# Moving the release of an expert's weight splits to GpSimd, and a second buffer for the rows of every other expert

## The chip, the cores and the metric

The kernel runs on one core of a Trainium2 chip. The metric is the device time of that core in microseconds (us), from launch to end. The profile is one execution of the same program, taken by the hardware profiler. Engines: TensorE (PE, with its weight loads as PEld), VectorE (DVE), ScalarE (ACT), GpSimd (POOL) and SyncE (SP, which issues the direct DMAs).

## The reference, cut to what matters

Two transformer layers over 512 tokens of width 1024 (with 256 context tokens). The second one ends in a mixture of eight experts, two for each token. All of the change lies in this last part:

```
def swiglu(x, w1, w3, w2):
    return (jax.nn.silu(x @ w1) * (x @ w3)) @ w2

def moe_swiglu(x, router, w1, w3, w2):
    ...
    logits = (xt @ router).astype(jnp.float32)
    top_v, top_i = lax.top_k(logits, TOP_K)
    top_w = jax.nn.softmax(top_v, axis=-1)
    gates = jnp.sum(jax.nn.one_hot(top_i, N_EXPERTS, dtype=jnp.float32) * top_w[..., None], axis=1)
    ...
    out = gates[:, 0:1] * swiglu(xt, w1[0], w3[0], w2[0])
    for e in range(1, N_EXPERTS):
        out = out + gates[:, e:e + 1] * swiglu(xt, w1[e], w3[e], w2[e])
```

w1, w3 are 1024x1408 and w2 is 1408x1024 for each expert. The result of the layer is the residual plus the gated output.

## The kernel before

**Weights.** Every matrix product is made of three float16 products: a float32 weight is scaled by 1024 and split into a high part (ACT, L283) and a low part (DVE, L288). A block of weights is a 128x2048 tile of w1 and w3 (11 of them for an expert, written j0 to j10 here) or a 128x1408 tile of w2 (8 of them, d0 to d7), so 19 blocks for an expert. `Stream` moves the blocks through two sets of buffers. A staging slot holds the float32 block as SP's DMA brings it (L260); it comes free when DVE has made the low part, and SP, which issues in order, then loads the next block into it. Before the change there are eight staging slots in this part: h (3), Kd (2), wst (2), Qc (1), named after the tensors whose space they use. A split slot holds the two float16 parts: whi/wlo (4), whix/wlox (1), aT (3). Splits run five blocks ahead of the block that TensorE multiplies (`LS1`). The first blocks of the first expert are split in four quarters of 512 columns.

**Experts.** They are taken in eight fixed places e0 to e7 with room for 176, 192, 96, 176, 112, 152, 136 and 128 tokens (e0 is expert 0, the others are ranked by load). `route` computes the top two, a position for every token, the one-hot matrices (ohs, L1707), from them by TensorE the token numbers (idxps, L1715), and as integers idx. `gather(e)` has GpSimd fetch an expert's tokens by indirect DMA into xg (one DMA for each group of up to 128 tokens, two for most experts). `prep` transposes xg on TensorE (xtp, L1858) and makes the float16 parts xT; for e0 it selects by one-hot matmuls instead (L1854), so that e0 needs no gather. `expert` runs the 11 blocks of w1 and w3 (L356), then the 8 of w2; the result comes back through ACT (my), a transpose (ytp) and DVE, which multiplies by the gate into the row buffers yr (L1927). `add_rows` has GpSimd add the finished rows into the output in DRAM by an indirect DMA (L2085). These DMAs follow each other: each waits until the one before it has landed. The tiles yr exist once (one for each group of tokens), so an expert's first rows wait until the DMAs of the expert before have read them.

**Order.** The order of instructions on each engine is decided at build time by the framework's scheduler, from data dependences and the order in which the code emits them; on the chip each engine then runs its list in that order and waits at the head of it. One dependence is put in by hand: for the first splits that `expert` asks for in e0 (j3 to j5 come under it), ACT's scale is not the constant 1024 but a tile `sw` that holds 1024, so that they can't be scheduled before `sw` is written:

```
        self.S.scale = self.ms.tile([128, 1], F32, name="sw")
        V.tensor_scalar(self.S.scale, pm[:, 0, 0:1], 0.0, SW, op0=OP.mult, op1=OP.add)
```

pm (L1691) holds the tokens' positions, which are known early in `route`. The blocks j0 to j2 and j7 are split before `route`.

Of the kernel before, what the change touches and what calls it, by code (L numbers as in the profile page):

```python
# [11 lines left out]
F32 = mybir.dt.float32  # L12
F16 = mybir.dt.float16
# [3 lines left out]
OP = mybir.AluOpType  # L17
# [4 lines left out]
D = 1024  # L22
# [12 lines left out]
CM = max(CAPS)  # L35
# [24 lines left out]
SW = 1024.0  # L60
# [146 lines left out]
def fixed_slot(kind, name, z):  # L207

    return kind, name, [z.bitcast(F32)] if kind == 'st' else [z[:, 0:2 * D], z[:, 2 * D:4 * D]]
# [110 lines left out]
class K:  # L320
# [1309 lines left out]
    def route(self, rp, pp, hook):  # L1630
        nc = self.nc
        V = nc.vector
# [19 lines left out]
        def t3(nm, dt=F32):  # L1652
            return rp.tile(b3, dt, name=nm)
# [36 lines left out]
        pm = t3("pm")  # L1690
# [26 lines left out]
        first = slots(0, lambda t: pm[:, t, 0:1])  # L1717

        self.S.scale = self.ms.tile([128, 1], F32, name="sw")
        V.tensor_scalar(self.S.scale, pm[:, 0, 0:1], 0.0, SW, op0=OP.mult, op1=OP.add)  # L1720
        hook([z[:, 0:CAPS[0]] for z in first])

        b77 = [128, 7, 7]
# [53 lines left out]
        for i, (s0, sn) in enumerate(self.slots[1]):  # L1777
            V.tensor_copy(self.idx[0:sn, 1, i:i + 1], ip[0:sn, 1, i, 0:1])
        self.gather(1)

        def rest(j):

# [83 lines left out]
                nc.vector.tensor_tensor(out=xT[:, 1, q, :], in0=af[:, q, :], in1=xT[:, 0, q, :], op=OP.subtract)  # L1866
        return xT

    def expert(self, C, slots, w13, w2, xT, mp, pp, done, wt=None, mid=None, nb=2, cm=CM, midj=6, beside=None):


        nc = self.nc
        CB = 256 if C <= 256 else 512
        gate = self.gate[3]
        gT = self.cut(mp.tile([128, 22 * cm], F16, name="mgT", tag="mgT", bufs=1), 22, C)
        gT = gT.rearrange("p (z k) c -> p z k c", z=2)
        prev, gf = [], [None]

        def evac():
            j, ps = prev.pop(0)  # L1880
            if j % 4 == 0:
                gf[0] = self.cut(mp.tile([128, 4 * cm], F32, name="mgf", tag="mgf", bufs=nb), 4, C)
            s = mp.tile([128, cm], F32, name="ms", tag="ms", bufs=2)[:, 0:C]
            nc.scalar.activation(s, ps[:, 0, 0:C], AF.Silu, scale=DESC)
            nc.vector.scalar_tensor_tensor(out=gf[0][:, j % 4, :], in0=ps[:, 1, 0:C], scalar=DESC * SA, in1=s, op0=OP.mult,  # L1885
                                           op1=OP.mult)
            if j in (3, 7, 10):
                q = slice(j // 4 * 4, j + 1)
                g = gf[0][:, 0:j % 4 + 1, :]
                nc.scalar.activation(gT[:, 0, q, :], g, AF.Copy)  # L1890
                nc.vector.tensor_tensor(out=gT[:, 1, q, :], in0=g, in1=gT[:, 0, q, :], op=OP.subtract)

        seg = [(0, C)]
        for j in range(11):
            wh, wl = (z.rearrange("p (j k c) -> p j k c", j=2, k=8) for z in w13(j))
            self.S.scale = SW
            ps = pp.tile([128, 2, CB], F32, name="mps", tag="m", bufs=3)
            for i in range(2):
                for k in range(KD):
                    self.mm1(ps[:, i], wh[:, i], wl[:, i], k, xT[:, 0], xT[:, 1], seg, k == 0, k == 7)  # L1900
            if prev:
                evac()
            prev.append((j, ps))
            if beside is not None:
                beside(j)
            if j == midj and mid is not None:
                mid()
        evac()
        yr = [mp.tile([128, D], F32, name="yr", tag=f"yr{s}", bufs=1) for s in range(len(slots))]
        py = []  # L1910

        def evac2():
            d, ps = py.pop(0)
            y = mp.tile([128, cm], F32, name="my", tag="my", bufs=nb)[:, 0:C]
            nc.scalar.activation(y, ps[:, 0, 0:C], AF.Copy, scale=gate[:, d, 0:1])  # L1915
            ys.append((d, y))

        def rows():
            d, y = ys.pop(0)
            tp = pp.tile([128, max(2, len(slots)), 128], F32, name="ytp", tag="t", bufs=2)  # L1920
            dd = slice(d * 128, (d + 1) * 128)
            for s, (s0, sn) in enumerate(slots):
                nc.tensor.transpose(tp[0:sn, s, :], y[:, s0:s0 + sn], self.ident)  # L1923
                if wt is None:
                    nc.vector.tensor_copy(yr[s][0:sn, dd], tp[0:sn, s, :])
                else:
                    nc.vector.tensor_scalar(yr[s][0:sn, dd], tp[0:sn, s, :], wt[0:sn, s:s + 1], None, op0=OP.mult)  # L1927
            done(d, yr)

        def part(w, ps, ks):  # L1930
            for k in ks:
                self.mm1(ps[:, 0], *w, k, gT[:, 0], gT[:, 1], seg, k == 0, k == 10)

        ys = []
        w0 = []
        for d in range(8):
            if d > 1 and len(ys) > nb - 1:
                rows()
            w = [z.rearrange("p (k c) -> p k c", k=11) for z in w2(d)]
            ps = pp.tile([128, 2, CB], F32, name="mps2", tag="m", bufs=3)  # L1940
            if d < 2 and nb > 1:

                part(w, ps, range(8))
                w0.append((w, ps))
                if d == 0:
                    continue
                for i in range(2):
                    part(*w0[i], range(8, 11))
                    py.append((i, w0[i][1]))
                evac2()  # L1950
                continue
            part(w, ps, range(11))
            if py:
                evac2()
            py.append((d, ps))
        evac2()
        while ys:
            rows()

    def overflow(self):  # L1960

# [71 lines left out]
    def moe(self, ctx):  # L2033
        nc, tc = self.nc, self.tc

        self.slots = [[(0, C // 2), (C // 2, C // 2)] if C > 128 else [(0, C)] for C in CAPS]
        self.eid = {}
        res = self.A['out'][0:NL].rearrange("(t p) c -> t p c", p=128)
        for t in range(4):
            nc.sync.dma_start(out=res[t], in_=self.h[:, t, :])  # L2040
        self.xg = {}
        with ExitStack() as c0:
            wx = c0.enter_context(tc.tile_pool(name="wx", bufs=1))
            self.S.extend(wx, 0, 1, fixed=self.wfix)
            self.S.ls = 4
            self.xgp = c0.enter_context(tc.tile_pool(name="xgp", bufs=1))
            rp = c0.enter_context(tc.tile_pool(name="rt", bufs=1))
            pp = c0.enter_context(tc.tile_pool(name="pm", bufs=1, space=PSUM))
            with ExitStack() as c:
                mp = c.enter_context(tc.tile_pool(name="mp", bufs=1))  # L2050
                first = []
                rest = self.route(rp, pp, lambda ohs: first.append(self.prep(CAPS[0], self.slots[0], None, mp, pp, ohs=ohs)))
                xT = first[0]

                B = [self.at3[:, 4 * D * z:4 * D * z + 4 * D] for z in range(3)]
                H = [self.ht[:, 2 * D * z:2 * D * z + 2 * D].bitcast(F16) for z in range(3)]
                self.S.extend(wx, 0, 1, fixed=self.wfix + [fixed_slot('hl', f"a{i}", z) for i, z in enumerate(B)]
                              + [fixed_slot('st', f"h{i}", z) for i, z in enumerate(H)])
                self.S.ls = LS1
                for e in range(NE):  # L2060
                    nxt = []

                    def mid():
                        if e + 2 < NE:
                            self.gather(e + 2)
                        if e + 1 < NE:
                            nxt.append(self.prep(CAPS[e + 1], self.slots[e + 1], self.xg.pop(e + 1), mp, pp))

                    self.expert(CAPS[e], self.slots[e], lambda j: self.S.get(('m13', e, j)), lambda j: self.S.get(('m2', e, j)),
                                xT, mp, pp, lambda d, yr: self.add_rows(e, d, yr), self.ws[:, e, :], mid, beside=None if e else rest)  # L2070
                    xT = nxt[0] if nxt else None
        self.kctx.close()
        self.overflow()
# [64 lines left out]
```

## Time and profile before

| | us |
|---|---|
| median of 3 runs | 1798.25 (1798.06 to 1801.5) |
| the profiled execution: its time | 1797.55 |
| its span, first to last instruction | 1795.8 |
| PE busy | 1654.4 (92%) |
| DVE busy | 1244.4 (69%) |
| ACT busy | 882.2 (49%) |
| mean granted TensorE clock | 0.975 |

The profiled execution takes 1.75 us more than its span, for what lies before the first and after the last instruction. The expert part lies between about 1288 us and the end. [...]

### The profile page before, as it was taken

The page shows a single profiled execution, that of the slowest core. Times are in us where ns is not written, and L with a number is a line of the kernel's source. Part 1 is how long each engine was busy: PE and PEld are TensorE (multiplying, and loading weights), DVE is VectorE, ACT ScalarE, POOL GpSimd, SP SyncE. Part 2 cuts the span into 40 slices and gives each one's busy share as a digit, 9 for nine tenths or more (in the row PEclk, how much of TensorE's full clock was granted, in tenths as well). Part 3 has the DMA queues.
Part 4 walks back from the last instruction along what each step waited for, and adds up shares of the span by engine and source line. Part 5 has one row for each costly group of instructions (what it writes and reads, how often), then busy time and mean ns, then how long its engine had stood idle before and what let it go on. Part 6 is the DMA issues. An engine that isn't in the chain of part 4 may idle for free. (4 is left out here: it accounts for less than half of the span.)

```text
span 1795.8 us, 36123 instructions
## 1 busy us (share of the span) xinstructions
PE 1654.4 (92%) x15124; PEld 1164.0 (65%) x15124; DVE 1244.4 (69%) x2397; ACT 882.2 (49%) x1420; POOL 155.0 (9%) x103
## 2 busy tenths in 40 slices
PE   3999999999999999999998999989669999999976
PEld 1444666555556666555555466457569988999976
DVE  6784899777664554233158999696867598787963
ACT  6564555253222222111255677565646587686762
POOL 1100000000000000000001000461130010010211
PEclk8999999999999999999999999999789999999988
DMA  8413242533443332233321202112468889999972
GB/s 324 156 51 108 98 162 95 213 116 141 141 141 139 124 137 96 72 112 112 115 92 60 83 1 72 71 48 90 168 208 306 267 287 359 324 363 326 314 251 48
DMA packets 53736, 286.83 MB, mean 160 GB/s; under 512 B 7760, under 2 KB 12880, under 8 KB 29504
## 3 DMA queue, kind: packets, MB, share of 16 engines
q1 hardware_dynamic: 47328, 271.74, 42.1%
q0 software_dynamic: 5232, 10.96, 2.9%
q8 instruction: 120, 1.97, 0.4%
q10 hardware_dynamic: 1008, 1.77, 0.3%
q14 instruction: 48, 0.39, 0.1%
HBM read 272.57 MB, written 11.08 MB: 158 GB/s over the span
## 5 line engine op out<-in xcount | busy, mean ns | idle before, releaser
L356 PEld LDWEIGHTS <-whi 128*128 128x128 f16 x5120 | 465.0, 98 | 184.5 <-issue 10.4
L356 PE MATMUL f<-yT,whi 128*128 128x512 f16 (+1 forms) x1408 | 325.5, 326 | 1.5 <-ACT af L452 1.5
L356 PEld LDWEIGHTS <-wlo 128*128 128x128 f16 x2560 | 251.7, 98 | 88.1 <-issue 0.4
L356 PE MATMUL f<-yT,wlo 128*128 128x512 f16 (+1 forms) x704 | 229.1, 326 | 0.0
L288 DVE SCALAR_TENSOR_TENSOR wlo<-wst,whi 128x2048 f16<-128x2048 f32 (+2 forms) x113 | 172.3, 1534 | 53.9 <-ACT whi L283 53.7
L283 ACT ACTIVATE whi<-wst 128x2048 f16<-128x2048 f32 (+2 forms) x115 | 147.0, 1299 | 89.0 <-PE f L356 71.9
L389 DVE SCALAR_TENSOR_TENSOR adjk<-wst,srow 128x1024 bf16<-128x1024 f32 x96 | 117.2, 1221 | 99.9 <-DMA wst<-in_w_adr_dram 98.8
L356 PE MATMUL f<-gT,whi 128*128 128x512 f16 (+1 forms) x704 | 164.4, 326 | 0.0
L356 PEld LDWEIGHTS <-aT 128*128 128x128 f16 x2376 | 153.6, 98 | 2.7 <-issue 2.2
L356 PE MATMUL mps<-xT,whi 128*128 128x176 f16 (+6 forms) x1408 | 142.3, 228 | 1.6 <-ACT xT L1865 1.3
L356 PE MATMUL mps<-xT,wlo 128*128 128x176 f16 (+6 forms) x704 | 136.6, 228 | 0.0
L288 DVE SCALAR_TENSOR_TENSOR wlo<-h,whi 128x2048 f16<-128x2048 f32 (+1 forms) x54 | 107.2, 1987 | 21.2 <-ACT whi L283 18.4
L356 PE MATMUL f<-gT,wlo 128*128 128x512 f16 (+1 forms) x352 | 114.7, 326 | 0.0
L283 ACT ACTIVATE whi<-h 128x2048 f16<-128x2048 f32 (+1 forms) x54 | 90.2, 1672 | 48.4 <-PE mps L356 46.6
L356 PE MATMUL mps<-xT,aT 128*128 128x112 f16 (+6 forms) x1584 | 105.5, 225 | 0.0
L481 DVE TENSOR_TENSOR h<-h,ytp 128x256 f32<-128x256 f32 (+1 forms) x48 | 24.3, 506 | 109.6 <-PE ytp L479 109.5
L356 PE MATMUL cvps<-aT,whi 128*128 128x512 f16 (+1 forms) x384 | 82.6, 328 | 2.8 <-ACT Kl L646 2.3
L288 DVE SCALAR_TENSOR_TENSOR aT<-wst,aT 128x2048 f16<-128x2048 f32 (+2 forms) x44 | 76.2, 1749 | 12.5 <-ACT aT L283 12.4
L1096 ACT CAST gT<-g 128x512 f16<-128x512 f32 (+1 forms) x23 | 14.0, 608 | 131.2 <-DVE g L1093 131.2
L356 PE MATMUL mps<-mgT,whi 128*128 128x176 f16 (+6 forms) x704 | 73.2, 229 | 1.4 <-DVE mgf L1885 0.9
L283 ACT ACTIVATE aT<-wst 128x2048 f16<-128x2048 f32 (+2 forms) x40 | 62.3, 1569 | 23.2 <-PE mps L356 22.0
L2085 POOL DMA_INDIRECT out_dram<-yr,sidx x14 | 41.9, 2989 | 336.6 <-DVE yr L1927 184.9
(405 smaller groups left out, 3404.7 us busy)
## 6 DMA issues: line engine op xcount, KB each, us to landing
wst<-in_w_adr_dram SPq DMA_DIRECT2D x32, 1024.0 KB, 4.9
h<-in_w_m_dram SPq DMA_DIRECT2D x30, 1024.0 KB, 9.4
wst<-in_w_m_dram SPq DMA_DIRECT2D x24, 1024.0 KB, 7.1
wst<-in_w_f_dram SPq DMA_DIRECT2D x22, 1024.0 KB, 4.9
Kd<-in_w_m_dram SPq DMA_DIRECT2D x22, 1024.0 KB, 7.2
h<-in_w_m_dram SPq DMA_DIRECT2D x24, 704.0 KB, 4.7
wst<-in_w_ada_dram SPq DMA_DIRECT2D x12, 1024.0 KB, 5.1
Qc<-in_w_m_dram SPq DMA_DIRECT2D x12, 1024.0 KB, 7.4
```

The lines of the kernel that those rows point to most:

```text
L283: nc.scalar.activation(h, x, AF.Copy, scale=self.scale)
L288: nc.vector.scalar_tensor_tensor(out=l, in0=x, scalar=SW, in1=h, op0=OP.mult, op1=OP.subtract)
L356: mm(ps[:, s0:s0 + sn], w[:, k, :], a[:, kk, s0:s0 + sn], start=first and p == 0, stop=last and p == 2)
L389: nc.vector.scalar_tensor_tensor(out=jk, in0=st[:, j * D:(j + 1) * D], scalar=1.0, in1=self.srow[:, t, :], op0=OP.mult, op1=OP.mult, accum ...
L481: nc.vector.tensor_tensor(out=hs, in0=hs, in1=tp[:, 0:w].rearrange("p (t c) -> p t c", t=nt), op=OP.add)
L1096: nc.any.tensor_copy(gh, g[:, 0:sn])
L2085: self.nc.gpsimd.indirect_dma_start(out=to, out_offset=bass.IndirectOffsetOnAxis(ap=self.sidx[0:sn, e, s:s + 1], axis=0), in_=yr[s][0:sn, ...
```

## The change

It has two parts. In `route` the tile `sw` is written by GpSimd instead of DVE, and the line stands behind `self.gather(1)`. And one of the three staging slots in h is given up: its space becomes two row buffers, which the experts with odd numbers use in place of yr. The function `rows` is renamed `back`, since `rows` is now an argument.

```
-        V.tensor_scalar(self.S.scale, pm[:, 0, 0:1], 0.0, SW, op0=OP.mult, op1=OP.add)
         hook([z[:, 0:CAPS[0]] for z in first])
...
         self.gather(1)
+        nc.gpsimd.tensor_scalar(self.S.scale, pm[:, 0, 0:1], 0.0, SW, op0=OP.mult, op1=OP.add)
...
-        yr = [mp.tile([128, D], F32, name="yr", tag=f"yr{s}", bufs=1) for s in range(len(slots))]
+        yr = rows or [mp.tile([128, D], F32, name="yr", tag=f"yr{s}", bufs=1) for s in range(len(slots))]
...
-                H = [self.ht[:, 2 * D * z:2 * D * z + 2 * D].bitcast(F16) for z in range(3)]
+                H = [self.ht[:, 2 * D * z:2 * D * z + 2 * D].bitcast(F16) for z in range(2)]
+
+                odd = [self.ht[:, (4 + z) * D:(5 + z) * D] for z in range(2)]
...
-                                xT, mp, pp, lambda d, yr: self.add_rows(e, d, yr), self.ws[:, e, :], mid, beside=None if e else rest)
+                                xT, mp, pp, lambda d, yr: self.add_rows(e, d, yr), self.ws[:, e, :], mid, beside=None if e else rest, rows=odd if e % 2 else None)
```

The scheduler's order moves with it. On GpSimd, at the start of the expert part (xg is the gathered tile, first of e1; L463 is the last work of the norm before; out_dram is the output, h_11901 the tile that now holds the odd experts' rows):

```order
 L463 TENSOR_TENSOR h_11901<-n_3_13527,aT_13066 128x512 x4
-L1833 DMA xg_13924<-n_d,idx 96x1024 x2
-L1833 DMA xg_14462<-n_d,idx 96x1024
-L1833 DMA xg_15539<-n_d,idx 88x1024 x2
-L2085 DMA out_dram<-yr,sidx 704x1024 x2
-L1833 DMA xg_16573<-n_d,idx 112x1024
-L2085 DMA out_dram<-yr,sidx 704x1024 x2
+L1779 TENSOR_SCALAR sw<-pm 128x1
+L1833 DMA xg_13923<-n_d,idx 96x1024 x2
+L1833 DMA xg_14461<-n_d,idx 96x1024
+L1833 DMA xg_15538<-n_d,idx 88x1024 x2
+L2087 DMA out_dram<-yr,sidx 704x1024 x2
```

The write of sw, though it stands behind gather(1) in the code, comes ahead of both of its DMAs in GpSimd's list: it needs only pm.

On ACT, in the same place (whix and the first aT are the splits of j3 and j4, xaf the output of e0's prep):

```order
-L283 ACTIVATE whix_13930<-Kd,sw 128x512
-L1862 ACTIVATE xaf<-xtp,nB_106,nA_102 128x176
-L283 ACTIVATE whix_13930<-Kd,sw 128x512 x2
+L1756 ACTIVATE ex<-ex 128x4
+L283 ACTIVATE whix_13930<-Kd,sw 128x512 x3
 L1862 ACTIVATE xaf<-xtp,nB_106,nA_102 128x176
 L283 ACTIVATE whix_13930<-Kd,sw 128x512
+L283 ACTIVATE aT_13066<-Kd,sw 128x512
+L1862 ACTIVATE xaf<-xtp,nB_106,nA_102 128x176
```

Three quarters of the split of j3 now stand ahead of the first xaf, where one stood; DVE's list changes alike (three low parts come early between the small operations of `route`).

On TensorE, within the blocks j0 to j2 of e0, which the scheduler interleaves (whi_13171 is j0, whi_13351 is j2; xg_13924 is e1's gathered tile):

```order
 L356 LDWEIGHTS whi_13351
 L356 MATMUL mps<-xT,whi_13351 128x176
-L1858 MATMUL xtp<-ident,xg_13924 128x96 x2
 L356 LDWEIGHTS whi_13171
 L356 MATMUL mps<-xT,whi_13171 128x176
```

The first two transposes of e1's tokens leave this place. In the list of the changed kernel they come only behind j6, 105 + 192 matmuls of e0 later, right ahead of j7 (whi_14095):

```order
+L1858 MATMUL xtp<-ident,xg_13923 128x96 x4
+L356 LDWEIGHTS whi_14095
+L356 MATMUL mps<-xT,whi_14095 128x176
+L356 LDWEIGHTS whi_14095
+L356 MATMUL mps<-xT,whi_14095 128x176
```

From e1 on the lists of TensorE, ACT and DVE are the same as before but for the names of the staging slots and of the row buffers.

## Rows read from the trace of the kernel before

**Rows 1.** The page: the span.

```profile
span 1795.8 us, 36123 instructions
```

**Rows 2.** The waits of TensorE, 1285 to 1796 us: total, times, longest.

```profile
PE ytp L1923 <- DVE yr L1927: 15.6, 15, 10.3
PE xtp L1858 <- DMA xg<-n_d,idx: 13.0, 1, 13.0
```

**Rows 3.** TensorE in order of time: start, us, instruction, [idle before <-releaser].

```profile
1305.32 0.39 PE L356 MATMUL mps<-xT,whi 128*128 128x176 f16 x3 [1.33 <-ACT xT L1865]
1318.76 0.58 PE L1858 MATMUL xtp<-ident,xg 96*128 96x96 f32 x2 [13.05 <-DMA xg<-n_d,idx]
1319.13 0.35 PE L356 MATMUL mps<-xT,whi 128*128 128x176 f16 x1
...
1329.01 0.31 PE L356 MATMUL mps<-xT,whix 128*128 128x176 f16 x2
...
1332.75 3.80 PE L356 MATMUL mps<-xT,aT 128*128 128x176 f16 x48
...
1336.73 3.80 PE L356 MATMUL mps<-xT,aT 128*128 128x176 f16 x48
```

**Rows 4.** After it: busy PE, PEld, DVE, ACT, POOL; clock, DMA, GB/s.

```profile
1318.76:1322.00 3.24, 3.24 (x22) 3.23 (x23) 0.00 (x0) 0.00 (x0) 0.00 (x0) 0.50 0.03 6
```

**Rows 5.** GpSimd in order of time: two gathers of e1, two additions of e5.

```profile
1302.23 11.73 POOL L1833 DMA_INDIRECT xg<-n_d,idx  x1 [13.40 <-DVE idx L1778]
1314.26 0.92 POOL L1833 DMA_INDIRECT xg<-n_d,idx  x1 [0.30 <-issue]
...
1677.40 12.78 POOL L2085 DMA_INDIRECT out_dram<-yr,sidx  x1 [58.03 <-DVE mgf L1885]
1707.90 1.82 POOL L2085 DMA_INDIRECT out_dram<-yr,sidx  x1 [17.71 <-DVE mgT L1891]
```

**Rows 6.** DVE in order of time, around the gather of e1.

```profile
1301.94 1.88 DVE L288 SCALAR_TENSOR_TENSOR wlox<-Kd,whix 128x512 f16<-128x512 f32 x3
...
1305.55 0.88 DVE L1866 TENSOR_TENSOR xT<-xaf,xT 128x704 f16<-128x704 f32 x1
...
1306.95 4.89 DVE L288 SCALAR_TENSOR_TENSOR aT<-wst,aT 128x512 f16<-128x512 f32 x8
1311.77 1.31 DVE L1707 TENSOR_SCALAR ohs<-cstm,pms 128x128 f16<-128x128 f32 x6
1326.35 0.15 DVE L1790 CAST idx<-idxps 96x1 int32<-96x1 f32 x1 [13.27 <-PE idxps L1715]
```

**Rows 7.** ACT in order of time, at the start of the splits under sw.

```profile
1293.42 0.72 ACT L283 ACTIVATE whix<-Kd,sw 128x512 f16<-128x512 f32 x1 [2.89 <-DVE sw L1720]
1294.41 0.50 ACT L1862 ACTIVATE xaf<-xtp,nB,nA 128x176 f32<-128x176 f32 x1 [0.28 <-PE xtp L1854]
```

**Rows 8.** DVE, then TensorE, in order of time, in the w2 blocks of e6.

```profile
1724.78 0.60 DVE L1927 TENSOR_SCALAR yr<-ytp,ws 68x128 f32<-68x128 f32 x2 [10.13 <-DMA out_dram<-yr,sidx]
1725.31 2.28 DVE L288 SCALAR_TENSOR_TENSOR wlo<-Qc,whi 128x2048 f16<-128x2048 f32 x1
1727.51 0.60 DVE L1927 TENSOR_SCALAR yr<-ytp,ws 68x128 f32<-68x128 f32 x2
...
1725.44 0.43 PE L1923 MATMUL ytp<-ident,my 128*68 128x128 f32 x1 [10.33 <-DVE yr L1927]
```

**Rows 9.** The columns of Rows 4, for a stretch of e3.

```profile
1505.00:1510.00 5.00, 5.00 (x69) 5.00 (x67) 4.45 (x3) 3.99 (x4) 3.29 (x1) 1.00 1.01 415
```

**Rows 10.** ACT: first and last of seven splits there, six held by loads.

```profile
1499.56 1.91 ACT L283 ACTIVATE aT<-wst 128x2048 f16<-128x2048 f32 x1 [1.12 <-DMA wst<-in_w_m_dram]
...
1515.69 1.38 ACT L283 ACTIVATE aT<-Kd 128x1408 f16<-128x1408 f32 x1 [1.11 <-DMA Kd<-in_w_m_dram]
```

**Rows 11.** DMA issues, 1260 to 1796 us: count, KB each, median us to landing.

```profile
h<-in_w_m_dram SPq DMA_DIRECT2D x29, 1024.0 KB, 9.2
```

**Rows 12.** A one-column GpSimd operation (L1804): ns min/median/max, first and last start.

```profile
L1804 POOL TENSOR_SCALAR own<-cstm x1: 192/192/192, 1234.7 to 1234.7; 128x1 f32<-128x1 f32 x1
```

More of the change, by code (lines that the diff above doesn't have):

```diff
@@ L1867, in prep, with expert @@
         return xT
-    def expert(self, C, slots, w13, w2, xT, mp, pp, done, wt=None, mid=None, nb=2, cm=CM, midj=6, beside=None):
+    def expert(self, C, slots, w13, w2, xT, mp, pp, done, wt=None, mid=None, nb=2, cm=CM, midj=6, beside=None, rows=None):
         nc = self.nc
@@ L1916, in evac2, with back @@
             ys.append((d, y))
-        def rows():
+        def back():
             d, y = ys.pop(0)
@@ L1937, in expert @@
             if d > 1 and len(ys) > nb - 1:
-                rows()
+                back()
             w = [z.rearrange("p (k c) -> p k c", k=11) for z in w2(d)]
@@ L1957, in expert @@
         while ys:
-            rows()
+            back()
     def overflow(self):
```

## The prediction

> **What bounds the kernel now.** I read the page first. TensorE is busy for 92% of the span of 1795.8 [rows 1], so only what makes TensorE idle, or slow, is worth time. Next I listed the waits of TensorE in the expert part [rows 2] and looked for long ones that this change touches. There are two, of one occurrence each: 13.0 for the gathered tokens of e1, and 10.3 for DVE's yr. Then I followed both in order of time on the engines concerned.
>
> The first is in [rows 3]. TensorE finishes the sums for e0's tokens, stands at the transposes of e1's tokens for 13.05, and goes on at 1318.76, inside j0 to j2 of e0. Those transposes are not urgent, since e1 is multiplied only after 16 more blocks of e0; they only stand early in the list. The gather came late because GpSimd's first indirect DMA took 11.73 where the next took 0.92 [rows 5]. DVE worked without a pause from 1301.94 to 1313.08 (the last of [rows 6] before its idle time), and the long DMA ended at 1313.96, 0.88 after DVE stopped. I read from these rows that a busy DVE holds back GpSimd's indirect DMAs. [...]
>
> The second is in [rows 8]. DVE waits 10.13 until e5's additions have read the rows that e6 wants to overwrite, and TensorE waits for DVE 10.33. The cause is in [rows 5]: e5's first addition was held 12.78 from 1677.40, again under a busy DVE, and its second, which follows it, was issued only at 1707.90.
>
> **Part one: sw on GpSimd.** The code reads as if the splits now waited until both gathers were issued. The order says otherwise: sw stands ahead of them, needs only pm, and GpSimd was idle for 13.40 ahead of the first gather [rows 5]. A one-column operation on GpSimd took 0.19 [rows 12]. So no hold, and DVE's splits still overlap the gather. The first split waited 2.89 for sw [rows 7]; with sw no longer behind DVE's list it can start that much earlier, and three quarters of j3 go ahead of xaf instead of one. TensorE had 0.28 of slack there, and two more quarters of some 0.6 on ACT can push the selection of e0's tokens back by up to 1; some of it is regained by the earlier start. I leave it at nothing and keep 1 in the lower bound.
>
> What does count is TensorE's order: the transposes of e1 leave their place and come behind j6. So TensorE runs on at once. DVE has xT ready at 1305.55 + 0.88 = 1306.43 [rows 6]. From there to the first product of j3 TensorE has 105 products of j0 to j2 and 12 small ones (idxps). A whole block of 48 products, with a few small ones, takes 3.74 or 3.98 at full clock [rows 3], so 105 take 105/48 of that, 8.2 to 8.7; I take 8.4, to 1314.8. One wait takes the place of the old one: the small products need the one-hots that DVE finishes at the end of its burst, at 1313.08 [rows 6], and the first of them stands behind 69 of the 105 products, at 1306.43 + 69 × 3.74/48 = 1311.8, or 1311.5 if the small ones are taken out of the 3.74. That is a wait of about 1.6. So j3 starts at 1306.43 + 8.4 + 1.6 = 1316.4, against 1329.01 before [rows 3]. [...] **Gain 12.6, taken as 12.5.** Bounds: if the clock falls anyway after the short wait (−1.5) and e0's selection comes 1 late, 10.1; if DVE's burst is done early and the 1.6 goes too, 14.2.
>
> The moved transposes are reached at 1316.4 + 3.74 + 3 × 3.98 = 1332.1. The gather landed at 1318.76 before; it starts perhaps 2 later now, but still ends when DVE's burst ends, so that I expect both landed by about 1319 to 1327 and no wait.
>
> **Part two: rows for odd experts.** e6 now writes the rows last used by e4, whose additions landed long before, so the wait of 10.13 goes. e5 and e7 use the odd rows in the same way. What is late next? DVE: behind the wait it has per block of w2 two operations on yr (0.60) and a split (2.28), and the starts of [rows 8] are 2.73 apart (1724.78 to 1727.51). TensorE was waiting for these. That cadence is the same after the change, just earlier, as the loads for those splits had long landed by then. **Gain 10.1**; 8 if DVE then runs into something I don't see, 10.3 by TensorE's own wait, and up to 1.5 more if the clock fell after this wait as it did after the other.
>
> **The price: seven staging slots in place of eight.** A staging slot less lets loads start one block later. That costs nothing where loads are early, and TensorE is behind a split lead of five blocks. It can cost where the DMA engines are full: between 1505 and 1510 they moved 415 GB/s with a share of 1.01 [rows 9], and ACT's splits around there waited for loads six times, 1.12, 1.11 and four between them of 0.5 to 0.6 [rows 10]. TensorE was busy for 5.00 of 5 there all the same, so the lead covers these waits. But a stretch which is bound by transfer drains the lead, and begins with one block less. A block of 1024 KB is 1.049 MB, at 415 GB/s 2.5. There are two such full stretches (this one, and one near 1600 to 1640), so the upper bound is 5 and the lower 0. As TensorE did not wait at the worst place, I am nearer to the lower end: **loss 1.0**.
>
> **Sum.** 1797.55 (the profiled time: the span of 1795.8 and 1.75 around it) − 12.5 − 10.1 + 1.0 = 1775.95. The median of the runs is 0.7 above the profiled execution, so 1776.6, and I say 1776. The bounds give 1797.55 − 14.2 − 11.8 + 0 + 0.7 = 1772.3 and 1797.55 − 10.1 − 8 + 5 + 0.7 = 1785.2.
>
> **Rivals.** *The gather is starved anyway.* DVE used to pause for 13.27 after its burst [rows 6], because TensorE stood still; GpSimd's second DMA fell into that pause. Now TensorE runs on, the pause shrinks to the time until the first small products are through (a microsecond or two), and DVE goes on with casts and splits. If the second DMA is held for as long as the first was, some 12, it is issued at about 1326 and lands 4.8 later (1318.76 − 1313.96) at 1331, just in time for 1332.1. If both are held, the second is out at 1339 and lands at 1344: a wait of 12, so 1788. For it: both long DMAs of [rows 5]. Against it: DVE's list has the casts behind TensorE's small products, so it must pause, and a pause of 0.92 is enough for a DMA. Chance 0.11, times 1778 to 1788. [...]
>
> *The slot costs its upper bound*, 5 in place of 1: 1780. For it: the DMA share of 1.01. Chance 0.07.
>
> *Only one gain comes*: the change does not do what it says about the splits, and if the first wait merely moves, 1776 + 12 = 1788; if e6 then waits for another thing, 1786. Chance 0.05.
>
> *Slower: seven slots are too few for the latency.* A slot is taken for the load, 9.2 from issue to landing [rows 11], then ACT's 1.91 [rows 10] and DVE's 2.28, in all about 13.4 and with some queueing 16. From j3 of e0 to the end TensorE has 16 + 133 blocks in 1795.8 − 1329.0, 3.13 each, so seven slots last 21.9. Should the cycle be 24, each of the 133 blocks of e1 to e7 would cost 24/7 − 3.13 = 0.30 more, 40 in all, and 1816. It decides as soon as a cycle exceeds 21.9; nothing but the full stretches comes near it. Chance 0.04. No change at all, from these together: 0.03.
>
> **Chances.** The likeliest case, both waits gone and a small price, has 0.7 and a range of its own of 1771 to 1781. With the starved gather, the dear slot and the single gain, the range that leaves out no more than 2 in 10 is 1769 to 1787. A difference of 0.2% (3.6) is about what a measurement of this kernel can tell from no change. Faster 0.92, same 0.03, slower 0.05.
>
> **What would show it.** Right: the waits of 13.0 and 10.3 are gone from TensorE's list; j3 starts near 1316; the clock stays at 1.00 through j0 to j2; a wait of a microsecond or two appears ahead of idxps; sw stands on GpSimd ahead of a first gather that is still about 10 long; ACT's waits for loads grow by a few us and TensorE's do not. Wrong: the transposes behind j6 wait for the gather; e6 waits for another DMA; TensorE's waits for DVE's or ACT's splits grow throughout e1 to e7, which would be the slot.

## The result, and the profile after

The median of the changed kernel is 1773.62 (4 runs, 1769.4 to 1774.93) against 1798.15 for the kernel before (4 runs, 1795.08 to 1801.5): a ratio of 0.9859, 95% interval 0.9835 to 0.9883, so 24.5 us less. The profiled execution took 1772.99, 24.56 less than the one of before.

The waits of TensorE after (total, times, longest), the counterpart of [rows 2]:

```profile
PE ytp L1923 <- ACT my L1915: 4.3, 6, 1.5
...
PE ytp L1923 <- DVE yr L1927: 2.8, 5, 1.3
PE ytp L1923 <- DVE h L1927: 2.7, 10, 0.5
...
PE idxps L1715 <- DVE ohs L1707: 0.5, 1, 0.5
```

Both long waits are gone (h is the name that the odd rows now bear), and no wait for xg is left. The engines around the old 13 us wait, in order of time, GpSimd first:

```profile
1292.62 0.19 POOL L1779 TENSOR_SCALAR sw<-pm 128x1 f32<-128x1 f32 x1 [3.50 <-DVE wd L1764]
1303.66 8.89 POOL L1833 DMA_INDIRECT xg<-n_d,idx  x1 [10.85 <-DVE idx L1777]
1312.85 0.92 POOL L1833 DMA_INDIRECT xg<-n_d,idx  x1 [0.30 <-DVE idx L1790]
1314.08 2.75 POOL L1833 DMA_INDIRECT xg<-n_d,idx  x1 [0.30 <-issue]
```

DVE:

```profile
1304.57 0.88 DVE L1866 TENSOR_TENSOR xT<-xaf,xT 128x704 f16<-128x704 f32 x1
...
1306.58 4.90 DVE L288 SCALAR_TENSOR_TENSOR aT<-wst,aT 128x512 f16<-128x512 f32 x8
1311.40 0.86 DVE L1707 TENSOR_SCALAR ohs<-cstm,pms 128x128 f16<-128x128 f32 x4
...
1312.86 0.98 DVE L1707 TENSOR_SCALAR ohs<-cstm,pms 128x184 f16<-128x184 f32 x4
1313.75 2.28 DVE L288 SCALAR_TENSOR_TENSOR wlo<-h,whi 128x2048 f16<-128x2048 f32 x1
```

TensorE, its waits and the starts of j3 (whix), j4, j5 and e1's transposes:

```profile
1305.51 0.24 PE L356 MATMUL mps<-xT,whi 128*128 128x176 f16 x1 [0.74 <-DVE xT L1866]
...
1311.73 0.18 PE L1715 MATMUL idxps<-rhs,ohs 128*128 128x4 f16 x1 [0.53 <-DVE ohs L1707]
...
1314.67 0.31 PE L356 MATMUL mps<-xT,whix 128*128 128x176 f16 x2
...
1318.41 3.80 PE L356 MATMUL mps<-xT,aT 128*128 128x176 f16 x48
1322.39 3.80 PE L356 MATMUL mps<-xT,aT 128*128 128x176 f16 x48
...
1330.11 0.53 PE L1858 MATMUL xtp<-ident,xg 96*128 96x96 f32 x4
```

The gather was not issued earlier: it starts at 1303.66 against 1302.23 [rows 5], and its first DMA is still held, 8.89. But nobody stands at it. TensorE goes on through j0 to j2, with waits of 0.74 and 0.53, and reaches the transposes at 1330.11, where the rows are there. The granted clock, a share of full speed, stays at 1.00, in place of the 0.50 of [rows 4]:

```profile
1306.00:1310.00 4.00, 4.00 (x56) 4.00 (x54) 4.00 (x8) 2.14 (x2) 4.00 (x1) 1.00 0.85 344
1310.00:1314.00 4.00, 3.47 (x48) 3.10 (x47) 3.98 (x15) 3.80 (x5) 3.47 (x2) 1.00 0.86 245
```

In e6's w2 blocks DVE now goes from block to block, 2.72 apart, with no wait in front of yr, the counterpart of [rows 8]:

```profile
1701.43 0.60 DVE L1927 TENSOR_SCALAR yr<-ytp,ws 68x128 f32<-68x128 f32 x2
1701.95 2.28 DVE L288 SCALAR_TENSOR_TENSOR wlo<-h,whi 128x2048 f16<-128x2048 f32 x1
1704.15 0.60 DVE L1927 TENSOR_SCALAR yr<-ytp,ws 68x128 f32<-68x128 f32 x2
```

and e5's additions are as late as before, 12.78 long and its second issued 30 after the first, only that no one needs their rows back:

```profile
1664.26 12.78 POOL L2087 DMA_INDIRECT out_dram<-h,sidx  x1 [58.04 <-DVE mgf L1885]
1694.30 1.82 POOL L2087 DMA_INDIRECT out_dram<-h,sidx  x1 [17.26 <-DVE mgT L1891]
```

**Where each microsecond came from.** Runs differ by some us in what lies ahead of the experts, so I count inside one trace: from DVE's first operation of `route` (lg, L1624: 1288.18 before, 1288.46 after) to ACT's start on the sums of a block (L1884 for j, L1915 for d). The table gives that time of before minus that of the run; "slots" is what is lost between e0's j10 and e6's d0, "e6" what comes in between e6's d0 and d7.

| run | e0 j10 | e3 j10 | e6 d0 | e6 d7 | slots | e6 |
|---|---|---|---|---|---|---|
| changed kernel | 14.40 | 13.88 | 13.43 | 24.06 | -0.97 | +10.63 |
| after_again (the same) | 14.38 | 14.36 | 14.14 | 24.77 | -0.24 | +10.63 |
| p1_sw_only | 15.12 | 15.12 | 15.11 | 14.32 | -0.01 | -0.79 |
| p2_rows_only | -1.35 | -1.94 | -1.97 | 8.66 | -0.62 | +10.63 |
| slot_only | 15.13 | 12.39 | 12.17 | 13.37 | -2.96 | +1.20 |
| slot_only_again | 14.39 | 13.66 | 13.29 | 14.18 | -1.10 | +0.89 |
| gather_late | 13.29 | 13.27 | 13.09 | 14.05 | -0.20 | +0.96 |
| gather_late_rows | 13.29 | 12.32 | 12.31 | 22.94 | -0.98 | +10.63 |
| sw_dve_late_line | 4.30 | 3.74 | 3.74 | 14.37 | -0.56 | +10.63 |
| true_hold | 8.39 | 6.11 | 6.12 | 16.75 | -2.27 | +10.63 |
| slots6 | 14.40 | 9.47 | 9.49 | 18.97 | -4.91 | +9.48 |
| slots5 | 15.12 | 11.05 | 8.24 | 14.80 | -6.88 | +6.56 |
| tt_splits | -1.05 | -1.05 | -1.06 | -1.57 | -0.01 | -0.51 |

For the changed kernel: 14.40 - 0.97 + 10.63 = 24.06, less the 0.28 by which `route` began later, plus some 0.8 behind the last rows, makes the 24.6 by which the span is shorter.

Two limits of this table. Its reference is a single trace: p2_rows_only and tt_splits, whose order on TensorE at e0 is that of before, stand at -1.35 and -1.05 there, so the gain at e0 is known to about 1.4. And that gain comes in two sizes, 14.4 and 15.1, even for one kernel (slot_only and slot_only_again). In slot_only, at 15.13, xT was ready 0.74 earlier than in the changed kernel, counted from the start of `route`. The products that select e0's tokens start 0.147 apart up to 1298.50 in the changed kernel, whose granted clock was 0.50 from 1297 to 1298; in p1_sw_only, at 15.12, they start 0.075 apart from 1295.67 on.

### The profile page after: what moved, and what is told of

Same layout as the page of the kernel before. It is cut to its first block, busy times and chain, and to the rows that moved or that the text cites. A ratio compares the mean times of both kernels' runs of the same rounds, so it can differ in the third digit from the quotient of the medians.

```text
span 1771.2 us, 36124 instructions
## 1 busy us (share of the span) xinstructions
PE 1652.8 (93%) x15124; PEld 1161.2 (66%) x15124; DVE 1244.0 (70%) x2395; ACT 883.1 (50%) x1421; POOL 155.3 (9%) x104
## 3 DMA queue, kind: packets, MB, share of 16 engines
q8 instruction: 120, 1.97, 0.5%
## 5 line engine op out<-in xcount | busy, mean ns | idle before, releaser
L288 DVE SCALAR_TENSOR_TENSOR wlo<-wst,whi 128x2048 f16<-128x2048 f32 (+2 forms) x132 | 210.4, 1603 | 58.3 <-ACT whi L283 58.1
L283 ACT ACTIVATE whi<-wst 128x2048 f16<-128x2048 f32 (+2 forms) x134 | 179.2, 1355 | 98.6 <-PE f L356 72.0
L356 PEld LDWEIGHTS <-aT 128*128 128x128 f16 x2376 | 153.7, 98 | 2.8 <-issue 2.2
L356 PE MATMUL mps<-mgT,wlo 128*128 128x176 f16 (+6 forms) x352 | 68.1, 227 | 0.0
L361 PEld LDWEIGHTS <-aT 128*128 128x128 f16 x384 | 38.4, 101 | 40.3 <-DVE aT L454 9.6
L363 PEld LDWEIGHTS <-aT 128*128 128x128 f16 x384 | 38.1, 100 | 39.9 <-issue 4.9
L1091 ACT ACTIVATE s<-f 128x512 f32<-128x512 f32 (+1 forms) x44 | 21.6, 491 | 83.5 <-PE f L356 83.4
L362 PEld LDWEIGHTS <-aT 128*128 128x128 f16 x384 | 38.4, 101 | 36.3 <-issue 9.5
```

Of the source, the lines that this page charges most:

```text
L283: nc.scalar.activation(h, x, AF.Copy, scale=self.scale)
L288: nc.vector.scalar_tensor_tensor(out=l, in0=x, scalar=SW, in1=h, op0=OP.mult, op1=OP.subtract)
L356: mm(ps[:, s0:s0 + sn], w[:, k, :], a[:, kk, s0:s0 + sn], start=first and p == 0, stop=last and p == 2)
L361: mm(ps, ah[:, kk, t0:t0 + 128], wh[:, k, :], start=first, stop=False)
L362: mm(ps, ah[:, kk, t0:t0 + 128], wl[:, k, :], start=False, stop=False)
L363: mm(ps, al[:, kk, t0:t0 + 128], wh[:, k, :], start=False, stop=last)
```

## The experiments

Behind each expectation stand the median of the run in us, its ratio to runs of the kernel before, and the 95% interval of that ratio.

**Each part alone.** p1_sw_only keeps the three slots in h and drops the odd rows; p2_rows_only puts sw back to DVE.

```
p1:  -H = [... for z in range(2)]        +H = [... for z in range(3)]
     -rows=odd if e % 2 else None
p2:  -nc.gpsimd.tensor_scalar(self.S.scale, ...)
     +V.tensor_scalar(self.S.scale, ...)      ahead of hook(...)
```

> Part one alone: sw on GpSimd, eight staging slots and one set of row buffers as before. If the two gains stand by themselves, j3 of e0 starts near 1314.7 as in the changed kernel, the wait of 10.3 in e6 is back, and the time is 14 below before, about 1784. Rival, that the smaller number of slots or the other space of the rows gave part of the early gain: well above 1784.

1781.21, ratio 0.9909 (0.9886 to 0.9932). 

> Part two alone: rows of the odd experts in the third h, seven slots, sw on DVE as before. If the parts are separate, the 13 us wait for the gather stays, the 10.3 us wait in e6 goes, and what the slot costs is in it: 11.3 less 1.6, with about 0.8 at the very end, so 10 to 11 below before, about 1788. Rival, that e6 only gained since it came 13 us earlier against something fixed in time: less than 5 below before.

1789.68, ratio 0.9956 (0.9941 to 0.9971). The parts are separate: 15.1 and -0.79 in e6 for the one, -1.35 and then 10.63 for the other. The medians are 16 and 7.5 below before and add to 23.5. The 7.5 is less than the 10 to 11 expected; in that trace 1.35 is lost at e0, with TensorE's order there unchanged.

**The price of a slot.** Part one with seven slots and no odd rows, twice:

```
-rows=odd if e % 2 else None        (and the list odd), H stays at range(2)
```

> Part one with seven slots, and the space of the eighth left unused (one set of row buffers). Beside the run with part one alone this prices the slot. If the loss of 14.06 to 13.12 that the two traces show between 1465 and 1640 is the slot, it comes back here: about 1 before e6, and up to 1.6 in all, so 1785 to 1786. Rival, that it came from the scheduler's new order or from the rows: the same time as part one alone within 0.3.

1783.83, ratio 0.9921 (0.9898 to 0.9943). 

> The run with part one and seven slots once more, for a second trace of the slot's price without the rows of part two, which was 2.96 up to e4 against 0.95 in the changed kernel. If the price hangs on the order that the list of slots takes with this kernel: 2.5 to 3.3 again. If on the execution: anything from 0.5 to 3.

1778.7, ratio 0.9903 (0.9884 to 0.9923). And the changed kernel once more: 

> The changed kernel once more, for a second trace. If the loss of about 0.95 between e2 and e4 is the slot's price as such, it comes out within 0.3 of that; if it hangs on how the loads of one execution fall, anything from 0.3 to 3. The first gap, up to e0's end, should be 14.4 again, and the time 1773 to 1775.

1772.5, ratio 0.9868 (0.9849 to 0.9886). The same kernel lost 2.96 and 1.10 in one case, 0.97 and 0.24 in the other, so the price hangs on the execution (the 0.24 lies just under the range given for that): 0.2 to 3 in the eight traces with seven slots, 0 to 0.2 in the three others with eight. Most of it falls in the stretch that was full of transfers before (e2's w2 and e3's first blocks; a DMA share of 0.97 to 1.04 from 1470 to 1530), where I looked for it.

**Fewer slots still.** range(2) in H becomes range(1) and range(0).

> The changed kernel with one staging slot in h instead of two: six in all. If a slot costs only in the stretches where transfers are full, some 1 to 2 again: 1774.5 to 1776. If slots are near to being bound by the time that one is taken (13 to 16 us against 6 times 3.13 = 18.8), still little, up to 4. A rival that each slot less shows as waits in every block: 15 or more.

1779.2, ratio 0.9908 (0.989 to 0.9926): 5.6 above the changed kernel, more than the 1 to 2 and the 4 expected, and far from 15. 

> The changed kernel with no staging slot in h: five in all. A cycle of 13 to 16 us against 5 times 3.13 = 15.7 is then at its limit: by the theory of the prediction's slow rival the loss jumps here, to 20 to 60 (1795 to 1835). By the rival that only the full stretches count, it stays at 3 to 6 (1777 to 1780).

1784.72, ratio 0.9946 (0.9931 to 0.9961). With six slots 4.9 are lost and e6 gains 1.15 less; with five it is 6.9, 4.1 and another 1.8 in e7. Neither of the two expectations for five held: no jump of 20 and more, but more than 3 to 6. The waits of TensorE with five slots, and ACT's waits for loads of which those come:

```profile
PE ytp L1923 <- ACT my L1915: 13.3, 11, 3.3
PE mps L356 <- DVE mgf L1885: 3.6, 7, 1.5
```

```profile
ACT whi L283 <- DMA Kd<-in_w_m_dram: 7.2, 5, 3.4
ACT whi L283 <- DMA wst<-in_w_m_dram: 5.6, 3, 4.1
ACT whix L283 <- DMA Kd<-in_w_m_dram: 2.8, 2, 1.6
```

They are few and long (11 waits for ACT, against 6 of 4.3 in all in the changed kernel, and not one in each of 133 blocks): at six of the seven that exceed 0.6, ACT, which has to bring back the results of w2 in order, has just stood at a split whose load had not landed. The price grows with every slot, from about 1 to 6 to 13 in all, without a threshold in this range.

**What gave the first gain: the place on TensorE.** In gather_late sw stays on DVE; the casts of e1's token numbers and the gather go into the work beside j1:

```
 def rest(j):
+    if j == 1:
+        for i, (s0, sn) in enumerate(self.slots[1]):
+            V.tensor_copy(self.idx[0:sn, 1, i:i + 1], ip[0:sn, 1, i, 0:1])
+        self.gather(1)
```

> The kernel before, with sw on DVE, but the two casts that make e1's token numbers, and the gather behind them, are written into the work beside block j1 of e0. By its order DVE makes those casts only after all the early splits, so the gather is issued near 1312, some 10 later than before, with no split to hold it; and the transposes of e1 come behind j6. If the place of the transposes on TensorE is what gave the gain, the 13 us wait goes although the gather is issued later: 12 to 14 below before, 1784 to 1786. Rival, that a gather issued or finished earlier is what counts: no gain, 1796 to 1800.

1782.92, ratio 0.9923 (0.9903 to 0.9943). GpSimd and TensorE of that run:

```profile
1308.42 1.34 POOL L1834 DMA_INDIRECT xg<-n_d,idx  x1 [23.22 <-DVE ohs L1707]
1310.06 3.42 POOL L1834 DMA_INDIRECT xg<-n_d,idx  x1 [0.30 <-DVE mgf L1886]
```

```profile
1327.32 0.53 PE L1859 MATMUL xtp<-ident,xg 96*128 96x96 f32 x4
```

`route` began 3.6 earlier here (1284.6), so the gather is issued 10 later than before, and still 13.29 is won: the transposes come behind j6, and the wait is gone. With the rows added: 

> The run with the late gather and sw on DVE as before, with part two added (rows of the odd experts, seven slots). If the two gains add: 13.3 and 10.6, less the slot's 1 to 3, so 22 to 24 below before, 1773 to 1776, the same as the changed kernel or 1 to 2 slower, since sw comes no earlier here. Rival, that moving both the gather and the rows collide: 1778 or more.

1774.56, ratio 0.9875 (0.9856 to 0.9894): the gains add, and it is as fast as the changed kernel within what this can tell.

The control, with sw on DVE at the new line:

```
-nc.gpsimd.tensor_scalar(self.S.scale, pm[:, 0, 0:1], ...)
+V.tensor_scalar(self.S.scale, pm[:, 0, 0:1], ...)
```

> The changed kernel with sw written by DVE instead of GpSimd, at the same place in the code, behind the gather of e1. By its order the transposes of e1 stand within j0 to j2 again. If the scheduler's place for them decides, the wait of about 13 for the gather is back and the time is 12 to 14 above the changed kernel, 1786 to 1788. Rival, that the line's place behind the gather does it, on any engine: 1773 to 1775.

1781.96, ratio 0.9923 (0.9906 to 0.9941).

```profile
1298.15 4.27 POOL L1833 DMA_INDIRECT xg<-n_d,idx  x1 [13.15 <-DVE idx L1777]
1302.72 1.02 POOL L1833 DMA_INDIRECT xg<-n_d,idx  x1 [0.30 <-DVE xT L1866]
```

```profile
1309.73 0.39 PE L1858 MATMUL xtp<-ident,xg 96*128 96x96 f32 x1 [9.62 <-DMA xg<-n_d,idx]
```

The wait is back, so the line in the code is not what counts. It is 9.62 and not 13, since here the first gather slipped through after 4.27; the expected number was missed by 4, between the two theories. So the time of the gather counts too, as long as the transposes stand early.

**The hold itself.** sw is computed from e1's token numbers; by the rows below it now stands behind both gathers:

```
+for i, (s0, sn) in enumerate(self.slots[1]):
+    z0, z1 = (0, 64) if i == 0 else (64, 128)
+    nc.gpsimd.tensor_scalar(self.S.scale[z0:z1], self.idx[0:64, 1, i:i + 1], 0.0, SW, ...)
```

> The changed kernel, but sw is computed from the token numbers of e1, so that GpSimd can write it only after both gathers are issued: the hold that the change's words speak of. If splits are what holds GpSimd, both gathers take about 0.9 and land near 1310 instead of near 1318. The splits start about 11 later, near 1304. By the theory that the gather's landing has slack to spare and that splits of 7 us fit before j3 to j5 need them: 1771 to 1776, like the changed kernel. Rival, that TensorE then waits for the late splits at j3 to j6: 3 to 8 slower, 1777 to 1782.

1778.03, ratio 0.9898 (0.9868 to 0.9928).

```profile
1303.88 2.95 POOL L1835 DMA_INDIRECT xg<-n_d,idx  x1 [14.96 <-DVE idx L1777]
1307.13 0.98 POOL L1835 DMA_INDIRECT xg<-n_d,idx  x1 [0.30 <-issue]
1308.19 0.45 POOL L1781 TENSOR_SCALAR sw<-idx 64x1 f32<-64x1 int32 x2
```

```profile
1308.68 2.56 ACT L283 ACTIVATE whix<-Kd,sw 128x512 f16<-128x512 f32 x4 [0.40 <-POOL sw L1781]
...
1316.15 1.28 ACT L1886 ACT_TABLE_LOAD   x1
1317.45 0.53 ACT L1886 ACTIVATE ms<-mps 128x176 f32<-128x176 f32 x2
```

```profile
1318.61 0.30 PE L356 MATMUL mps<-xT,whix 128*128 128x176 f16 x1 [4.58 <-DVE mgf L1887]
```

The order of the rows: GpSimd, then ACT, then TensorE. The gather is done by 1308.1 in place of 1313.8 (its first DMA took 2.95, with quarters of a split that doesn't depend on sw, j6's, beside it). The scheduler's order is another one here: the transposes of e1 stand between j0 to j2 and j3, and TensorE finds the rows there with a wait of only 0.65:

```profile
1312.61 0.30 PE L1860 MATMUL xtp<-ident,xg 96*128 96x96 f32 x1
1313.57 0.47 PE L1860 MATMUL xtp<-ident,xg 96*128 96x96 f32 x3 [0.65 <-DMA xg<-n_d,idx]
```

So a gather that is early enough is a second way out of the wait of 13, and this kernel still gains 8.39 by e0's j10. What it loses comes next. The splits, now in one piece from 1308.68 on, stand ahead of ACT's and DVE's work on j0's sums, and TensorE waits 4.58 for the space of these sums, and then starts its products 0.147 apart from 1319.44 to 1322.08, against 0.076 from 1322.50 on. (The 22 products of [rows 4] in 3.24, at a granted clock of 0.50, are 0.147 apart too.) The rival was right in its time, though TensorE waits for the sums behind the splits and not for the splits: 6.0 less than the changed kernel at e0's j10, and 4.4 in the medians of the two (four runs of 1774.64 to 1783.57, so the 6.0 is the firmer number).

**What holds GpSimd.** In the kernel before, the low parts of j3 to j6 of e0 as a plain subtraction:

```
+if key[0] == 'm13' and key[1] == 0 and 3 <= key[2] <= 6:
+    nc.vector.tensor_tensor(out=l, in0=x, in1=h, op=OP.subtract)
```

> The kernel before, with the low parts of j3 to j6 of e0 (the twelve and four early quarter splits of DVE) written as a plain subtraction of two tensors, which leaves out the scale of 1024, so those four blocks' values differ; order and sizes stay. In the run with sw on DVE behind the gather, a gather was finished while DVE ran the plain subtraction that makes xT. If it is the scaled form of the split that holds GpSimd, the first gather of e1 takes 1 to 2 instead of 11.7 and lands 8 to 10 earlier, so the wait of 13 falls to 3 to 6: 1787 to 1790. Rival, that any work of DVE holds it: 11 to 13 again and the time of before, 1796 to 1799.

1796.01, ratio 1.0001 (0.9989 to 1.0013).

```profile
1304.36 10.97 POOL L1836 DMA_INDIRECT xg<-n_d,idx  x1 [13.29 <-DVE idx L1781]
1315.63 0.92 POOL L1836 DMA_INDIRECT xg<-n_d,idx  x1 [0.30 <-issue]
```

The form of the split makes no difference that shows, 10.97 against 11.73. But "any work of DVE" falls as well, by the rows of the changed kernel above: the second gather took 0.92 from 1312.85 to 1313.77, while DVE ran little but one-hots; the first ended at 1312.55, 1.07 after the last early split and in the middle of other DVE work; the third ended at 1316.83, 0.80 after the split that it had met. So the long holds, 8.89 in the changed kernel, 10.97 and 11.73, lie under splits, and under one-hots a gather took 0.92 here.

That a split holds every such DMA is not shown; two rows speak against it. In sw_dve_late_line the second gather took 1.02 from 1302.72 on (above), while DVE ran scaled splits without a pause and at their usual distance of 0.60. (The first, which my expectation put down to xT's plain subtraction, ended in the first of these splits, 0.07 after that subtraction.) DVE in that run:

```profile
1302.27 0.68 DVE L288 SCALAR_TENSOR_TENSOR aT<-Kd,aT 128x512 f16<-128x512 f32 x1
1302.88 4.89 DVE L288 SCALAR_TENSOR_TENSOR aT<-wst,aT 128x512 f16<-128x512 f32 x8
```

And an addition of the changed kernel took 1.64 within one long split; its last one, from 1762.06 with DVE idle, took 1.56:

```profile
1376.65 2.36 DVE L288 SCALAR_TENSOR_TENSOR wlox<-wst,whix 128x2048 f16<-128x2048 f32 x1
1376.69 1.64 POOL L2087 DMA_INDIRECT out_dram<-yr,sidx  x1 [38.81 <-issue]
```

What decides between the long holds and the 1.02 and 1.64 stays open.

## Why the prediction was right, point by point

**The first term** was right in its mechanism and too small: 12.5, bounds 10.1 to 14.2, against 14.40, just above the upper bound. The failing steps are two. xT was ready at 1305.45 and not at 1306.43: I kept e0's selection where it was, with a possible loss of 1; in fact it came 0.98 earlier (1.26 counted from the start of `route`), though three quarters of j3 go ahead of it. ACT makes the high parts of xT in two steps (L1865). The first starts 9.96 after the start of `route` in both kernels; ahead of it ACT now does six quarter splits in place of four, so that six of some 0.6 in place of eight stand between it and the second, which comes 1.22 earlier. The earlier sw made room for that. It came 0.9 earlier and not the 2.89 that I read from [rows 7]: ACT still waits for it, since sw needs pm, which DVE finished only at 1292.24 in the kernel before. (The slack of 0.28 in those rows was ACT's, not TensorE's.)

```profile
1292.84 1.95 ACT L283 ACTIVATE whix<-Kd,sw 128x512 f16<-128x512 f32 x3 [2.03 <-POOL sw L1779]
```

The run gather_late, where sw stays on DVE and this does not happen, gains 13.29, 1.1 less than the changed kernel. And the wait that I put ahead of idxps at 1.6 was 0.53: I let TensorE wait for the end of DVE's burst, but its first small product needs only the first of the one-hots behind the last split, and that split ended at 1311.48. From the first product to j3 it took 1314.67 - 1305.51 = 9.16, so 8.6 without that wait, where I had 8.4. The 1.5 for the clock in the lower bound is the 9.88 that 105 products took from 1319.13 to 1329.01 [rows 3], the clock at 0.50 in the first part [rows 4], less the 8.4; no run shows it behind a wait as short as this, and behind the 0.53 the clock was 1.00.

**That the announced hold does not happen** was right: sw stood at 1292.62, 11 ahead of the gather, and a true hold is slower. But I treated a hold only as something that would not happen: true_hold shows that it does make the gather fast and does end the wait of 13, and that the late splits then cost more than the changed kernel pays.

**The starved gather** (my rival with 0.11) did not come, and its premise was partly wrong: I took any busy DVE to be the cause, so that a pause was needed. DVE had none, and the second gather still took 0.92. That one-hots and not splits met it I had not foreseen, so its timing was luck in part.

**The second term** was right: 10.1 forecast, 10.63 in each of the traces with odd rows and seven slots, the wait of 10.33 and a little of what lay around it.

**The slot** was sized well within its bounds of 0 to 5: 1.0 forecast, 0.97 and 0.24 measured in the changed kernel, with 2.96 as the most that seven slots cost in any trace. That 0.97 meets 1.0 is luck, since the eight traces spread from 0.24 to 2.96. And I took it from 1505 to 1510 alone that TensorE does not wait in the full stretch; between 1495 and 1500, in e2's w2 blocks, it was busy for 3.73 of 5 with a DMA share of 1.01, and it is in these blocks that the losses begin. The slow rival (a cycle longer than the slots last) was wrong about its shape, too: six and five slots cost 6 and 13, by long waits at few places.

**The sum:** 1775.95 for the profiled execution against 1772.99. Of the 3.0, 1.9 is the first term, 0.5 the second, and the rest lies ahead of `route` and behind the last rows.

**What stays open.** Why the first gather of before ended 2.1 after the last early split [rows 5, 6], where 1.07 to 1.55 is seen in the traces with sw on GpSimd, why it slipped through after 4.27 in sw_dve_late_line, and why some of these DMAs pass beside a split, I can't tell from these traces. Why the price of a slot differs between executions of one kernel was not tried either.

## What to carry to other kernels

TensorE, which runs its list in order, stood for 13.05 at transposes that nobody needed yet [rows 3]. Before making a late transfer earlier, look whether the instruction that waits for it can stand later; here that gave 13 to 15 us with the transfer as late as ever. In the two runs whose gather was done 5 to 6 earlier than in the changed kernel (true_hold, sw_dve_late_line) the transposes stood early, and 8.4 and 4.3 were gained in place of 14.4. Where a scheduler places the work, an edit on one engine (a one-column write) can move the work of another, so the lists are to be compared before the times are argued. And a buffer that is taken from one use for another is to be priced in the stretch where transfers are full, by one less and two less.

## What the runs showed of the hardware that I had not expected

A busy DVE did not hold every indirect DMA of GpSimd. Under runs of splits single ones took 8.89 (the changed kernel), 10.97 (tt_splits, whose early splits are plain), 11.73 and 12.78 (the kernel before); under one-hots one took 0.92 (the changed kernel). And not every DMA under splits was held: one took 1.02 (sw_dve_late_line), one 1.64 (the changed kernel).
